# A transformer block on one core: the list scheduler's order taken from its finer model of the engines

## The chip, the cores and the metric

The kernel runs on 1 core of one Trainium2 chip. The metric is the device time of one execution in microseconds (us), the median over runs. The core has five engines with an instruction queue each: TensorE (PE, matrix products; its weight loads stand as PEld in the profile), VectorE (DVE), ScalarE (ACT), GpSimd (POOL) and SyncE (SP, which here issues nearly all transfers). An engine takes its instructions in the order of its queue, and waits at the head of it for the semaphores that the instruction names.

## The reference, cut to what matters

One block over 2048 tokens of width 1024, in float32:

```python
h = rmsnorm(x, norm_mix_g)
q, k, v, u, vg = split(h @ w_in)                  # 1024 x 2560
a_out = stick_breaking_attention(q, k, v)         # 8 heads of 64, strictly causal
b_out = spatial_gating(gelu(u), gelu(vg), ...)    # 8 groups, 128 x 128 position mixing
mix = concat(rmsnorm(a_out, g_a), rmsnorm(b_out, g_b))
x = x + mix @ w_out                               # 1024 x 1024
h = rmsnorm(x, norm_mlp_g)
x = x + square(relu(h @ w_up)) @ w_down           # 1024 x 4096 x 1024
return rmsnorm(x, norm_final_g)
```

In the attention, the weight of key s for query t is sigmoid(z_ts) times the product of (1 - sigmoid(z_tj)) over the keys j between s and t: a running product along the keys, from the last to the first.

## The kernel before, in words

**The arithmetic.** Every large product is made from operands that are split in two parts, high and low (`split`, lines 78 to 85: ACT writes the high part at line 81 or 84, DVE subtracts it and writes the low part at line 82 or 85), and three passes on PE: high by high, high by low, low by high (`mm3`, lines 89 to 91). One pass multiplies a 128 x 128 tile into 512 columns.

**Stages.** Tokens go in four chunks of 512. `proj` (line 109) makes the projections, first of chunks 0 and 1 together, then of chunk 2 and of chunk 3; the split weights `w_in` are kept in DRAM (`wi_d`) after their first use and loaded from there later, and q, k and v go out to DRAM. `attention` (line 316) is a generator of small steps. A step works on 128 queries against 512 keys of one head: `weigh` loads the keys `kt` (line 329, 2 buffers), the values `vt` (line 331, 3 buffers) and the queries `qt`, makes the scores `z` on PE (lines 345, 346, and 348 on the diagonal), two sigmoids on ACT (`kk` at 351, `b` at 353), the running product `pr` on DVE (a scan, lines 356 and 359) and the weights `b` by a product on DVE (357 and 360). Five steps later `turn` transposes them on PE (line 370) and splits them into `aT`, and two steps after that `gather` multiplies them with `vt` into `av` (lines 388 and 389). `Out` (line 462) takes a chunk's attention and gating results back from DRAM, splits and transposes them (`operands`; 32 matmuls of one column against a column of ones, line 498, sum the squares of the attention output for its norm, whose mean is taken by the DVE instruction `ra_m` at line 73), multiplies them with `w_out` (`product`) and normalizes and transposes the result (`turn`, line 567). The MLP runs plainly for chunks 0 and 1 (`up_plain`, `down_plain`) and, for chunks 2 and 3, by a scheme with seven products in the place of eight (`up_seven`, `down_seven`, with operands from `Rights` and `Lefts`).

**Order in the program.** `together` (line 916) walks through two generators, a main one and the attention as a side one, and takes a given number of side steps (1.0, 0.5 or 0.49) for each main one. So the program text interleaves projection with attention of earlier chunks, then `Out` with attention, then the plain MLP with attention.

**Order on the engines.** The text isn't yet the order of the queues. When the `with tile.TileContext(...)` block of `kernel` closes, the library's list scheduler walks through the program on a model of the engines: whenever an engine of the model is free, it takes the first instruction in the order of the text whose operands the model holds to be finished and whose buffers it holds to be free. The order in which the model took them is the order of the engine's queue on the chip, for all five queues, SP's transfers included; semaphores are placed afterwards, so that the result is right whatever the order. Instructions that the model held to be ready early so stand early, and if on the chip their operands come later, what is behind them waits. The library has two such models: a coarse one, which is the default, and a finer one that it otherwise uses to simulate the timeline of a finished program.

## Time and profile before

| | us |
|---|---|
| median of 3 runs | 2582.65 |
| the three runs | 2588.75, 2582.65, 2582.36 |
| the profiled execution's own time | 2588.74 |
| its span, from the first to the last instruction | 2587.0 |
| PE busy in the span | 2461.0 |
| DVE busy | 1709.0 |
| ACT busy | 1152.8 |
| moved by DMA | 446.58 MB |
| mean granted share of PE's full clock | 0.974 |

Busy time is the time in which an engine had an instruction in execution; matmuls overlap each other, so the time of one matmul is longer than the distance between two. A row of a timeline gives start, duration, engine, line and operation, and in brackets the idle time of the engine before it with the instruction that ended it.

### The profile page before, as it was taken

The page shows a single profiled execution, that of the slowest core. Times are in us where ns is not written, and L with a number is a line of the kernel's source. Part 1 is how long each engine was busy: PE and PEld are TensorE (multiplying, and loading weights), DVE is VectorE, ACT ScalarE, POOL GpSimd, SP SyncE. Part 2 cuts the span into 40 slices and gives each one's busy share as a digit, 9 for nine tenths or more (in the row PEclk, how much of TensorE's full clock was granted, in tenths as well). Part 3 has the DMA queues.
Part 4 walks back from the last instruction along what each step waited for, and adds up shares of the span by engine and source line. Part 5 has one row for each costly group of instructions (what it writes and reads, how often), then busy time and mean ns, then how long its engine had stood idle before and what let it go on. Part 6 is the DMA issues. An engine that isn't in the chain of part 4 may idle for free.

```text
span 2587.0 us, 30340 instructions
## 1 busy us (share of the span) xinstructions
PE 2461.0 (95%) x11424; PEld 2001.7 (77%) x11424; DVE 1709.0 (66%) x2280; ACT 1152.8 (45%) x2004; POOL 307.6 (12%) x255
## 2 busy tenths in 40 slices
PE   8899999998989999999999899999988999999997
PEld 7687677776867888888878688888877888778886
DVE  3743448867668666666666788745557666577787
ACT  4432335546345555555563554422235445433333
POOL 1100001100010000000000000000013232223331
PEclk9999999999989999999999999999999999999999
DMA  9736787678664343433363733255323444573422
GB/s 373 245 130 208 226 258 247 196 215 280 220 216 150 115 127 115 126 119 118 122 208 136 255 115 118 85 211 207 136 82 130 153 152 151 216 260 127 163 98 98
DMA packets 158225, 446.58 MB, mean 173 GB/s; under 512 B 12544, under 2 KB 28928, under 8 KB 138624
## 3 DMA queue, kind: packets, MB, share of 16 engines
q1 hardware_dynamic: 149744, 417.39, 48.4%
q0 software_dynamic: 4032, 25.17, 2.4%
q10 hardware_dynamic: 4304, 2.10, 0.3%
q8 instruction: 90, 1.47, 0.2%
q14 instruction: 55, 0.45, 0.1%
HBM read 314.59 MB, written 130.02 MB: 172 GB/s over the span
## 4 chain that ended last, share of the span: by engine, by line
PE 77%; DVE 13%; DMA 3%; issue 2%; ACT 2%; POOL 2%; SPq 0%; POOLq 0%; DVEq 0%; ACTq 0%
PE mm L91 21%; PE mm L90 21%; PE mm L89 21%; PE tr L370 4%; PE av L388 2%; PE av L389 2%; PE z L346 2%; PE z L345 2%; DVE pr L359 2%; DVE w L82 2%; DVE pr L356 1%; DVE aT L82 1%; DVE t L82 1%; DMA w_in<-wi_d 1%; PE mm L498 1%
## 5 line engine op out<-in xcount | busy, mean ns | idle before, releaser
L91 PE MATMUL mm<-t,t 128*128 128x512 f32 x1280 | 504.4, 394 | 0.0
L90 PE MATMUL mm<-t,t 128*128 128x512 f32 x1280 | 503.9, 394 | 0.2
L89 PE MATMUL mm<-t,t 128*128 128x512 f32 x1280 | 503.0, 395 | 0.2 <-DVE t L663 0.2
L351 ACT ACTIVATE kk<-z 128x512 f32<-128x512 f32 (+2 forms) x320 | 171.4, 536 | 359.3 <-PE z L346 242.6
L359 DVE TENSOR_TENSOR_SCAN pr<-kk,pr,zeros 128x513 f32<-128x513 f32 x192 | 247.0, 1287 | 121.2 <-ACT kk L351 120.8
L91 PEld LDWEIGHTS mm<-t,t 128*128 128x128 f32 x1280 | 242.7, 190 | 52.5
L90 PEld LDWEIGHTS mm<-t,t 128*128 128x128 f32 x1280 | 242.8, 190 | 52.3 <-DVE t L85 1.0
L89 PEld LDWEIGHTS mm<-t,t 128*128 128x128 f32 x1280 | 242.8, 190 | 52.1 <-DVE t L663 0.6
L81 ACT ACTIVATE aT<-tr 128x512 fp32r<-128x512 f32 (+1 forms) x320 | 172.6, 541 | 124.1 <-PE tr L370 123.8
L370 PE MATMUL tr<-ident,b 128*128 128x128 f32 x1088 | 184.4, 282 | 34.0 <-DVE aT L82 21.6
L82 DVE TENSOR_TENSOR aT<-tr,aT 128x512 fp32r<-128x512 f32 (+1 forms) x320 | 191.3, 599 | 35.9 <-ACT aT L81 35.7
L370 PEld LDWEIGHTS tr<-ident,b 128*128 128x128 f32 x1088 | 133.3, 143 | 79.0 <-DVE aT L82 28.1
L90 PE MATMUL mm<-w,w 128*128 128x512 f32 x448 | 176.5, 394 | 10.7 <-DVE w L82 9.1
L91 PE MATMUL mm<-w,w 128*128 128x512 f32 x448 | 175.4, 392 | 0.0
L89 PE MATMUL mm<-w,w 128*128 128x512 f32 x448 | 172.6, 391 | 2.3 <-ACT w L81 2.3
L353 ACT ACTIVATE b<-z 128x512 f32<-128x512 f32 (+2 forms) x320 | 170.8, 534 | 0.0
L81 ACT ACTIVATE t<-t 128x1024 fp32r<-128x1024 f32 x104 | 105.5, 1063 | 134.4 <-DMA t<-in_w_down 68.0
L356 DVE TENSOR_TENSOR_SCAN pr<-kk,zeros 128x128 f32<-128x128 f32 (+3 forms) x128 | 104.5, 819 | 88.1 <-ACT kk L351 87.5
L82 DVE TENSOR_TENSOR w<-raw,w 128x512 fp32r<-128x512 f32 (+1 forms) x135 | 152.4, 1130 | 3.3 <-ACT w L81 2.8
L81 ACT ACTIVATE w<-raw 128x512 fp32r<-128x512 f32 (+1 forms) x135 | 106.4, 800 | 105.3 <-PE mm L91 85.8
L91 PE MATMUL mm<-t,w 128*128 128x512 f32 x380 | 149.7, 394 | 3.5 <-DVE w L82 3.5
L89 PE MATMUL mm<-t,w 128*128 128x512 f32 x380 | 150.7, 397 | 0.1
(214 smaller groups left out, 4776.8 us busy)
## 6 DMA issues: line engine op xcount, KB each, us to landing
w_in<-wi_d SPq DMA_DIRECT2D x40, 1024.0 KB, 7.8
kt<-k_d SPq DMA_DIRECT2D x160, 256.0 KB, 5.0
t<-in_w_down SPq DMA_DIRECT2D x28, 1024.0 KB, 5.2
s_d<-acts SPq DMA_DIRECT2D x16, 1792.0 KB, 6.2
raw<-s_d SPq DMA_DIRECT2D x28, 1024.0 KB, 4.8
t<-wo_d SPq DMA_DIRECT2D x24, 1024.0 KB, 7.1
wi_d<-w_in POOLq DMA_DIRECT2D x20, 1024.0 KB, 8.3
vt<-v_d SPq DMA_DIRECT2D x80, 256.0 KB, 2.7
```

What stands on the lines that cost most here:

```text
L81: nc.scalar.activation(hi, src, AF.Copy)
L82: nc.vector.tensor_tensor(lo, src, hi.bitcast(F32), ALU.subtract)
L89: nc.tensor.matmul(ps, lh, rh, start=first, stop=False, skip_group_check=more)
L90: nc.tensor.matmul(ps, lh, rl, start=False, stop=False, skip_group_check=more)
L91: nc.tensor.matmul(ps, ll, rh, start=False, stop=last, skip_group_check=more)
L345: nc.tensor.matmul(z[:, :Z], ql, kt[:, 0, :Z], start=True, stop=False)
L346: nc.tensor.matmul(z[:, :Z], ql, kt[:, 1, :Z], start=False, stop=not diag)
L351: nc.scalar.activation(kk[:, :L], z[:, :L], AF.Sigmoid, scale=-QK_SCALE)
L353: nc.scalar.activation(b[:, :L], z[:, :L], AF.Sigmoid, scale=QK_SCALE)
L356: nc.vector.tensor_tensor_scan(pr[:, L - 1::-1], kk[:, L - 1::-1], zeros[:, :L], 1.0, ALU.mult, ALU.add)
L359: nc.vector.tensor_tensor_scan(pr[:, ::-1], kk[:, ::-1], zeros, carry[tb], ALU.mult, ALU.add)
L370: nc.tensor.transpose(tr[:, tb * P:(tb + 1) * P], bs[tb][:, j * P:(j + 1) * P], ident)
```

## The change

The scheduler's model is exchanged: one argument where the context is opened. No line of the block itself changes.

```diff
-    with tile.TileContext(nc) as tc:
+    with tile.TileContext(nc, schedule_with_timeline_sim=True) as tc:
         block_kernel(tc, *args)
```

## Rows read from the trace of the kernel before

**Rows 1.** The page's first part: busy time, share of the span, instructions.

```profile
PE 2461.0 (95%) x11424; PEld 2001.7 (77%) x11424; DVE 1709.0 (66%) x2280; ACT 1152.8 (45%) x2004; POOL 307.6 (12%) x255
```

**Rows 2.** Stretches: length; PE, PEld, DVE, ACT, POOL busy (count); PEclk, DMA share, GB/s.

```profile
0.00:250.00 250.00, 231.19 (x1025) 189.53 (x1026) 117.86 (x188) 93.55 (x136) 25.74 (x51) 0.98 0.67 238
250.00:600.00 350.00, 324.62 (x1578) 256.16 (x1576) 224.25 (x384) 153.82 (x329) 23.64 (x29) 0.98 0.76 233
600.00:850.00 250.00, 221.41 (x1057) 178.26 (x1057) 189.20 (x277) 128.61 (x258) 20.14 (x24) 0.90 0.63 205
850.00:1350.00 500.00, 496.62 (x2461) 408.27 (x2459) 323.88 (x414) 286.91 (x547) 11.45 (x13) 1.00 0.41 128
1350.00:1480.00 130.00, 117.89 (x548) 94.53 (x547) 88.96 (x119) 55.21 (x101) 5.20 (x7) 0.91 0.63 212
1480.00:1920.00 440.00, 439.22 (x2055) 362.85 (x2054) 287.44 (x368) 148.34 (x238) 18.30 (x23) 0.99 0.40 138
1920.00:1960.00 40.00, 25.76 (x93) 19.03 (x92) 31.12 (x35) 21.28 (x30) 14.30 (x11) 0.86 0.28 106
1960.00:2250.00 290.00, 290.00 (x1260) 237.33 (x1259) 180.72 (x239) 142.63 (x240) 78.52 (x57) 1.00 0.44 159
2250.00:2587.00 337.00, 314.27 (x1360) 255.72 (x1359) 265.59 (x261) 122.45 (x131) 110.32 (x40) 0.98 0.41 154
```

**Rows 3.** Timeline of PE, 355 to 358 us.

```profile
355.60 0.47 PE L89 MATMUL mm<-w_in,hT 128*128 128x512 f32 x1
...
357.44 0.33 PE L370 MATMUL tr<-ident,b 128*128 128x128 f32 x1 [0.90 <-DVE b L357]
357.53 0.48 PE L89 MATMUL mm<-w_in,hT 128*128 128x512 f32 x1
357.85 0.39 PE L90 MATMUL mm<-w_in,hT 128*128 128x512 f32 x1
```

**Rows 4.** PE's waits: us in total, times, longest us.

```profile
PE tr L370 <- DVE aT L82: 21.6, 23, 1.8
PE tr L370 <- DVE b L357: 9.8, 16, 1.5
...
PE z L345 <- DMA kt<-k_d: 7.4, 2, 3.8
```

**Rows 5.** Timeline of DVE, 752 to 754 us.

```profile
752.12 0.16 DVE L73 TENSOR_SCALAR ra_m<-mm 128x4 f32<-128x4 f32 x1 [6.72 <-PE mm L498]
752.20 0.28 DVE L357 TENSOR_TENSOR b<-b,pr 128x127 f32<-128x127 f32 x1
752.40 1.55 DVE L356 TENSOR_TENSOR_SCAN pr<-kk,zeros 128x256 f32<-128x256 f32 x2
```

**Rows 6.** Timeline of PE, 745 to 753 us.

```profile
745.27 6.82 PE L498 MATMUL mm<-ones,t 128*128 128x1 f32 x32
...
752.52 0.63 PE L90 MATMUL mm<-t,t 128*128 128x512 f32 x1
```

**Rows 7.** Line 498, who waited for it: us in total, times.

```profile
  DVE ra_m L73: 24.1, 4
```

**Rows 8.** The chain that ended last, line 498, three of four: start, us.

```profile
645.49 6.62 PE mm L498 x32
...
1353.83 6.62 PE mm L498 x32
...
1704.17 4.12 PE mm L498 x32
```

**Rows 9.** Timeline of all engines around 1935 us.

```profile
1934.18 2.36 DVE L82 TENSOR_TENSOR t<-w,t 128x1024 fp32r<-128x1024 f32 x2 [3.38 <-DMA out_y<-t]
```

**Rows 10.** Waits of SP's queue: us in total, times, longest us.

```profile
SPq L331 <- PE av L389: 411.2, 58, 24.5
```

**Rows 11.** Timeline of all engines, 617 to 631 us.

```profile
617.64 7.17 SPq L329 DMA_DIRECT2D kt<-k_d  x2
...
630.89 0.55 PE L345 MATMUL z<-kt,qt 128*128 128x256 f32 x1 [3.79 <-DMA kt<-k_d]
```

## The prediction

> **What bounds the kernel now.** Read first the page's table of engines [rows 1]: TensorE (PE) is busy 2461.0 of 2587.0 us. All that better cover could give back is therefore the remaining 126.0 us and what the clock cost. Then read the stretches [rows 2], cut where the stages change. They fall into two kinds. From 850 to 1350, 1480 to 1920 and 1960 to 2250 us PE is busy 496.62 of 500, 439.22 of 440 and 290.00 of 290 us: 4.16 us idle in 1230. No order of its instructions can shorten these unless it shortens the work, and the work is the same. The idle time lies in the others: 18.81 us in 0 to 250, 25.38 in 250 to 600, 28.59 in 600 to 850, 12.11 in 1350 to 1480, 14.24 in 1920 to 1960 and 22.73 in 2250 to 2587. In the third and fourth the granted clock is 0.90 and 0.91 as well: part of the time PE ran at the lower of its two levels, 1.2 instead of 2.4 GHz.
>
> Then ask of each idle piece: was other work ready on the same engine, placed behind the instruction that waited? Only those pieces can change when the order does. The timeline of PE shows the pattern [rows 3]: a transpose of the attention (line 370) waits 0.90 us for VectorE's (DVE's) product `b`, and directly behind it stand passes of a projection whose operands had been in use since 355.60. The scheduler puts nothing on an engine that its model says isn't ready while something else is. So its model had the transpose's operand done sooner than the chip did.
>
> **The change, part by part.** It adds and removes no instruction, no byte and no buffer; every engine keeps its work. It changes the time at which the scheduler believes each result is there, and so the order on five queues, SP's DMAs included. Its cost is the sum of the waits that it moves.
>
> (a) *Transposes placed too early.* PE waited 21.6 us (23 times) at line 370 for the split half `aT` and 9.8 us (16 times) for `b` [rows 4], 31.4 us together. Not all have something ready behind them. Around 730 to 745 the operands of the next matmuls are themselves late (DVE is busy 189.20 of 250 us there, a larger share than in any other stretch but the two short of full at the end [rows 2]), so moving a transpose back would only move the wait. In 250 to 600, where the projection's weights are mostly resident, the wait goes. The ends are 0 (all waits are real dependences) and 31.4 us; I take a third, 10 us, since the stretch 250 to 600 holds about a quarter to a third of the idle time outside the start-up and the tail.
>
> (b) *DVE held by one small instruction.* In the operand stage of each `Out`, 32 matmuls of one column (line 498) sum the squares of the attention output. They take 6.82 us [rows 6], and DVE's 0.16 us instruction `ra_m` stands at the head of its queue for 6.72 of them [rows 5], though a product `b` and two scans stand right behind and need nothing from those matmuls: they run at once when it is through, 0.28 and 1.55 us, 1.8 together. This happens 4 times, 24.1 us in all [rows 7]. A model that prices 32 such matmuls at what they take would put the scans first. By the chain of waits [rows 8] the first of the four lies at 645 us, the third at 1354 and the last at 1704; the second is that of [rows 6]. The first three lie in stretches where DVE limits PE, the fourth where PE is full. In each of the three between 1.8 us (the rows shown) and the whole wait, some 6, would be done earlier. Ends: 0 and 3 x 6 = 18 us. I take 6, a third, near the rows shown (3 x 1.8 = 5.4): PE works in that time anyway, and only what it waits less afterwards counts.
>
> (c) *The clock.* In 600 to 850 and 1350 to 1480 the granted shares of 0.90 and 0.91 mean that 20% of 250 and 18% of 130 us, 73 us, were at the lower level; if PE worked throughout, half of that, 37 us, is what it cost. The level shows in one pass of 512 columns, which takes 0.63 us in [rows 6] and 0.39 in [rows 3]. Fewer waits could win some of it back; a worse order could lose as much. Ends: 37 us won, 37 lost. I take 0, because the work around the falls stays: the clock is low after the 6.82 us of line 498 [rows 6], in which PE was busy, with one column at a time.
>
> By the Trainium skill's TensorE: Matmul & The Clock Gate, section HAM oscillation, idle gaps between bursts bring the lower clock back and its price is half of the time spent there; by that rule, a third of the waits gone would give a third of (c) too, 12 us more, and the sum below would be 28 instead of 16. The trace agrees on the two levels (0.63 and 0.39 us a pass); against the idle gaps as the only cause stand the 6.82 busy us of line 498, after which the clock is low.
>
> (d) *The start-up, the change of stage at 1930 and the tail.* Here I cost the change at nothing. At 1934 DVE waits 3.38 us for an output's DMA to free a buffer [rows 9], in the stretch with 14.24 us of idle PE: a dependence, not an order. Ends: these 3.38 us won, if the buffer is given out in another order, and as much lost.
>
> (e) *SP's queue.* SP is the one queue where an instruction that waits holds many others: it stood 411.2 us at line 331 until a `vt` buffer was free [rows 10]. Today this reaches PE in two waits for `kt`, 7.4 us [rows 4]. A new order of DMAs can change this in either direction: ends 7.4 won and, below, 22 lost; I take 0.
>
> Sum: 10 + 6 = 16 us, 0.6%. The profiled execution's own time is 2588.74 us (span 2587.0 and 1.7 around it); the median of the three runs shown is 2582.65, 6.1 lower. So 2588.7 - 16 = 2572.7 for an execution like the profiled one and 2566.6, rounded 2567, for the median.
>
> **The rivals.** 0.3%, 7.7 us, is about what a measurement of this kernel can tell from no change.
>
> *No change within that.* The order may differ in many places, yet the waits are dependences and buffers: the transposes wait for DVE whatever the order, `ra_m` hides behind line 498 in which PE works anyway. For: nearly half of the kernel, the 1230 us with 4.16 idle, can't move, and DVE at 189.20 of 250 us has little room where it matters. Against: [rows 3] and [rows 5], where ready work stood behind. Also here: the two models may agree on every order that counts, so that the change does nothing. Time: 2582.65 less 0 to 7, say 2580. The Trainium skill's Perfetto Trace Analysis, section Optimization Strategy, reads a gap that repeats on the engine that should be full as a sign of too few buffers for the next tile; the trace agrees in part: SP's 58 waits for a `vt` buffer [rows 10] are such gaps, and an order leaves the number of buffers alone. I give this case 0.25.
>
> *Slower: loads of `kt` behind a waiting `vt`.* The place is SP's queue between 250 and 850 us, where projections and attention share it. The mechanism shows once, in [rows 11]: the issue of two halves of `kt` takes from 617.64 until 624.81, because SP was held in between, and PE idles 3.79 us until 630.89, when the second has landed. If the finer model issues the `vt` loads (3 buffers) a little earlier relative to `kt` (2 buffers), this wait repeats; each costs 3.7 us (7.4 by 2). It decides from the third added wait if nothing is won in (a) and (b) (11.1 us, over the 7.7), from the seventh if the 16 us are. With six and nothing won: 2582.65 + 22 = 2605. For it: SP waits at line 331 in 58 cases already, so little is needed. Against it: a model closer to the chip should rather see the held queue. I give slower by over 0.3% 0.28.
>
> *Much faster.* All of (a) and (b) and a third of (c): 31.4 + 18 + 12 = 61 us, 2522. This needs every wait to have ready work behind it, and [rows 9] and the DVE share in [rows 2] speak against. It is within the chance of faster, at 0.05.
>
> **How the numbers follow.** Faster by over 0.3% has 0.47: 0.42 for the forecast and 0.05 for the much faster case; no change 0.25; slower 0.28. The forecast's own range is 2545 (the upper ends of (a) and half of (b) and (c) lie beyond it) to 2575. The range over all cases goes from 2543 to 2606: it takes in the slower rival at six waits and leaves out the much faster case and a slower one with more than six.
>
> **What would show it.** Right: in the changed profile PE's waits at line 370 fall from 31.4 towards 20 us; DVE's wait at `ra_m` before line 498's end falls from 24.1 towards 5 with scans or products run in those 6.8 us; the stretches 850 to 1350 and the like keep their lengths, and the gain sits in the stages that are 250 to 850 and 1350 to 1480 now. Wrong: if PE's waits for `kt` or `w_in` grow past 20 us, the slower rival holds; if the waits fall and the span doesn't, they were only moved; if the full stretches change their length, the order reached work that I took as fixed.

## The result, and the profile after

The changed kernel takes 2517.15 us (median of 4 runs, 2511.05 to 2518.97) against 2583.74 (4 runs, 2582.36 to 2588.75; the three shown ahead of the prediction had 2582.65) for the kernel before: a ratio of 0.9731, with a 95% interval of 0.9716 to 0.9745. It is 66.6 us faster; the forecast was 16, and 2517 lies below the range. The profiled execution took 2518.97 us. The first part of its page, against [rows 1]:

```profile
PE 2430.1 (97%) x11424; PEld 1991.5 (79%) x11424; DVE 1694.0 (67%) x2280; ACT 1145.2 (45%) x2004; POOL 309.8 (12%) x255
```

The same instructions; PE is busy 30.9 us less, and idle 87.1 us of 2517.2 in place of 126.0. The mean granted clock is 0.982 (before 0.974).

To see where the time came from, both traces are cut at the ends of the same matmuls, so that each stretch holds the same work on PE. First the kernel before (columns as in [rows 2]): the gates (the columns for u and vg in the first projections) of chunks 0 and 1, the projections of chunks 2 and 3 with the attention beside them, everything behind them.

```profile
52.70:163.70 111.00, 99.33 (x450) 81.49 (x450) 62.14 (x107) 44.25 (x65) 12.76 (x17) 0.95 0.58 204
253.90:611.70 357.80, 332.46 (x1616) 262.98 (x1617) 234.93 (x397) 160.37 (x341) 24.11 (x30) 0.98 0.75 230
611.70:2577.30 1965.60, 1893.43 (x8770) 1546.42 (x8768) 1351.32 (x1691) 895.97 (x1523) 256.65 (x172) 0.97 0.45 154
```

Then the same three in the changed kernel:

```profile
53.90:148.60 94.70, 94.70 (x451) 79.25 (x450) 61.73 (x108) 44.04 (x64) 13.37 (x20) 1.00 0.61 231
238.80:559.30 320.50, 316.28 (x1616) 260.20 (x1617) 234.86 (x398) 158.08 (x339) 28.36 (x30) 0.99 0.79 257
559.30:2506.70 1947.40, 1882.42 (x8769) 1540.52 (x8768) 1336.26 (x1687) 890.44 (x1522) 252.40 (x171) 0.98 0.45 155
```

The gates of the start-up fall by 16.3 us (15.1 of it are left at the end of the first projections, 253.9 to 238.8), the projections of chunks 2 and 3 by 37.3, and the other 1966 us by 18.2. That is 70.6 us and not 66.6, because it compares the two profiled executions, and that of the kernel before took 5 us more than its median. In the second stretch PE's idle time falls from 25.3 us (357.80 less 332.46) to 4.2.

PE's waits in the changed kernel, against [rows 4]:

```profile
PE tr L370 <- DVE aT L82: 17.8, 18, 2.2
...
PE z L345 <- DMA kt<-k_d: 2.7, 2, 1.6
...
PE tr L370 <- DVE b L357: 1.8, 2, 0.9
```

The transposes' waits for `aT` and `b` fall from 31.4 to 19.6 us. The 436.3 us that SP's queue stands at `vt`, against [rows 10], are more than before:

```profile
SPq L331 <- PE av L389: 436.3, 69, 21.3
```

Who waited for line 498, against [rows 7]:

```profile
  DVE ra_m L73: 8.0, 3
```

That wait falls from 24.1 to 8.0 us. Yet the stretches in which the first three of [rows 7] lay shrink little: the output products of chunks 0 and 1 by 1.8 us (218.9 to 217.1), that of chunk 2 by 3.1 (98.0 to 94.9). First the one of chunks 0 and 1 before, then in the changed kernel:

```profile
611.70:830.60 218.90, 190.31 (x917) 152.75 (x916) 163.14 (x246) 111.91 (x226) 18.75 (x22) 0.90 0.66 216
```

```profile
559.30:776.40 217.10, 186.66 (x909) 149.63 (x909) 160.44 (x243) 111.47 (x226) 16.07 (x22) 0.90 0.65 218
```

### The profile page after: what moved, and what is told of

Read it like the earlier page. It is cut to its first block, busy times and chain, and to the rows that moved or that the text cites. A ratio compares the mean times of both kernels' runs of the same rounds, so it can differ in the third digit from the quotient of the medians.

```text
span 2517.2 us, 30341 instructions
## 1 busy us (share of the span) xinstructions
PE 2430.1 (97%) x11424; PEld 1991.5 (79%) x11424; DVE 1694.0 (67%) x2280; ACT 1145.2 (45%) x2004; POOL 309.8 (12%) x255
## 4 chain that ended last, share of the span: by engine, by line
PE 86%; DVE 8%; issue 3%; DMA 3%; ACT 1%; POOL 0%; POOLq 0%; SPq 0%; DVEq 0%; ACTq 0%
PE mm L91 24%; PE mm L90 24%; PE mm L89 23%; PE tr L370 4%; PE av L389 2%; PE z L346 2%; PE av L388 2%; PE z L345 2%; DVE w L82 2%; DVE t L82 1%; DVE pr L359 1%; PE mm L498 1%; DVE aT L82 1%; PE mm L263 1%; DMA t<-b_d 1%
## 5 line engine op out<-in xcount | busy, mean ns | idle before, releaser
L82 DVE TENSOR_TENSOR aT<-tr,aT 128x512 fp32r<-128x512 f32 (+1 forms) x320 | 191.1, 598 | 21.6 <-ACT aT L81 21.3
L370 PE MATMUL tr<-ident,b 128*128 128x128 f32 x1088 | 180.9, 279 | 21.9 <-DVE aT L82 17.8
L90 PE MATMUL mm<-w,w 128*128 128x512 f32 x448 | 176.4, 394 | 8.8 <-DVE w L82 8.6
L91 PE MATMUL mm<-w,w 128*128 128x512 f32 x448 | 175.6, 392 | 0.0
L82 DVE TENSOR_TENSOR t<-t,t 128x1024 fp32r<-128x1024 f32 x104 | 123.6, 1225 | 39.1 <-ACT t L81 19.4
```

Source lines behind the costliest of these rows:

```text
L82: nc.vector.tensor_tensor(lo, src, hi.bitcast(F32), ALU.subtract)
L90: nc.tensor.matmul(ps, lh, rl, start=False, stop=False, skip_group_check=more)
L91: nc.tensor.matmul(ps, ll, rh, start=False, stop=last, skip_group_check=more)
L370: nc.tensor.transpose(tr[:, tb * P:(tb + 1) * P], bs[tb][:, j * P:(j + 1) * P], ident)
```

## The experiments

**How an order is moved from one kernel to the other.** Both kernels trace the same instructions in the same order; only the queues differ. So the order that the finer model gave one queue can be written into the kernel before as a chain: each instruction of the queue must be issued behind the one ahead of it, with no wait for its end. The scheduler's model then lists the other queues around that, so their orders can change as well: a run that holds one queue doesn't change that queue alone. The edit, the same in all runs named pin_ or free_ (the text of an order is left out):

```diff
+ORDERS = {
+    "SP": "...",
+}
+
+def forced_order(tc):
+    traced = tc.nc.cur_bb.bb.instructions
+    for text in ORDERS.values():
...
+        for first, then in zip(order, order[1:]):
+            tc.add_manual_dep(then, first.name, mybir.DependencyInfo(
+                mybir.DependencyClass.NoSync, mybir.DependencyReason.DATA), reason="order")
...
         together(down_seven(loads, rm))
+    forced_order(tc)
```

All runs in one table. Start is the end of the first projections, the second column the stretch with the projections of chunks 2 and 3, the third the rest up to the last matmul, from the profiled execution and cut at the same matmuls as above (in ra_11 more attention falls into the second). Ratios are to the kernel before on the same chip.

| run | us | ratio, 95% interval | start | proj 2, 3 | rest |
|---|---|---|---|---|---|
| before (profiled) | | | 253.9 | 357.8 | 1965.6 |
| changed (profiled) | 2517.15 | 0.9731, 0.9716 to 0.9745 | 238.8 | 320.5 | 1947.4 |
| pin_sp | 2584.06 | 0.9992, 0.9983 to 1.0002 | 251.6 | 344.3 | 1983.8 |
| pin_pe | 2635.79 | 1.0192, 1.0176 to 1.0208 | 252.9 | 375.5 | 1988.2 |
| pin_act | 2616.04 | 1.0121, 1.0105 to 1.0137 | 247.1 | 359.4 | 1994.8 |
| pin_dve | 2625.05 | 1.0153, 1.0138 to 1.0168 | 254.8 | 354.8 | 2001.7 |
| pin_all | 2522.02 | 0.9751, 0.9734 to 0.9767 | 238.7 | 322.6 | 1949.9 |
| free_pe | 2565.43 | 0.9926, 0.9911 to 0.9941 | 243.4 | 328.3 | 1979.3 |
| free_sp | 2607.49 | 1.0088, 1.0073 to 1.0103 | 243.8 | 389.7 | 1963.9 |
| free_dve | 2545.67 | 0.9846, 0.9831 to 0.9860 | 241.2 | 326.2 | 1961.4 |
| pair_act_sp | 2566.42 | 0.9920, 0.9905 to 0.9935 | 244.4 | 330.8 | 1974.4 |
| pin_first | 2570.24 | 0.9937, 0.9923 to 0.9952 | 238.4 | 359.3 | 1964.5 |
| pin_proj | 2551.08 | 0.9867, 0.9851 to 0.9884 | 253.6 | 323.5 | 1958.3 |
| pin_late | 2566.14 | 0.9916, 0.9902 to 0.9931 | 253.2 | 355.5 | 1947.3 |
| stores_pool | 2576.04 | 0.9961, 0.9946 to 0.9976 | 253.6 | 343.0 | 1963.7 |
| win_pool | 2599.50 | 1.0044, 1.0027 to 1.0061 | 255.1 | 363.9 | 1968.1 |
| split_pool | 2591.42 | 1.0022, 1.0012 to 1.0032 | 259.2 | 356.5 | 1964.6 |
| undo_sp | 2554.98 | 0.9877, 0.9858 to 0.9897 | 239.1 | 358.4 | 1949.9 |
| stores_fine | 2518.55 | 0.9744, 0.9730 to 0.9759 | 238.9 | 321.3 | 1944.1 |
| ra_11 | 2520.40 | 0.9738, 0.9723 to 0.9752 | 238.8 | 329.8 | 1934.5 |

**One queue at a time.** The theories were: SP (loads behind waiting stores), PE (transposes placed too early, as the prediction had it), ACT, and joint.

```diff
+    "SP": "...",      # pin_sp; "PE", "ACT" or "DVE" in its place for the other three
```

> The kernel before (coarse model), with SyncE's queue alone held to the order that the finer model gave it; the coarse model lists the other four engines around that. Theory SP (loads stood behind waiting stores on SyncE's queue, so attention's k and v blocks came late and in bursts): the stretch of proj of chunks 2 and 3 falls from 356 us to about 320, the start-up of the gates stays at 111, in all 2535 to 2550 us. Theory PE (the transposes stood too early in TensorE's own queue): that stretch stays within 5 us of 356, in all 2575 to 2585. Theory ACT (ScalarE's order alone): no change here. Theory joint (no one engine's order carries it): under 10 us, 2573 to 2585.

> The kernel before, with TensorE's queue alone held to the finer model's order. Theory PE: the waits of the transposes on aT and b (31.4 us) go, and the stretch of proj of chunks 2 and 3 falls from 356 us to about 320; the gates' start-up stays; in all 2535 to 2550 us. Theory SP: the loads are as late as before, so TensorE waits elsewhere (for k blocks and scores) and the stretch stays above 345; in all 2570 to 2590. Theory ACT: no change. Theory joint: under 10 us either way, or some us slower.

> The kernel before, with ScalarE's queue alone held to the finer model's order. Theory ACT (in the gates of chunks 0 and 1 a weight's split stood ready behind a sigmoid that waited for VectorE): that stretch falls from 111 us to about 96; in the stretch of proj of chunks 2 and 3 nothing, in all about 2568 us. If ScalarE's order carries the later stretch too: 2530 to 2545. Theory SP or PE for the start-up: the stretch stays at 108 to 111, in all 2578 to 2585.

> The kernel before, with VectorE's queue alone held to the finer model's order. If the gates' start-up hangs on VectorE's order (evacuations before or after the multiplications that the sigmoids wait for): that stretch falls from 111 us to about 96, in all about 2568. If the scans of the attention steps were bunched by VectorE's own order: the stretch of proj of chunks 2 and 3 falls by 20 us or more, in all 2550 or below. By theories SP, PE and ACT: within 5 us of 2583.

No queue brings the gain alone, and three of the four make the kernel slower; these three totals lie outside every range that was written down for them. SP's order wins 13.5 us in the projections of chunks 2 and 3 and loses 18.2 behind them; ScalarE's wins 6.8 us in the start-up, half of what is to be had there. PE's order is the telling one. Its waits in the stretch of 375.5 us:

```profile
PE z L364 <- DMA qt<-q_d: 31.7, 2, 18.2
PE mm L108 <- DMA w_in<-wi_d: 11.9, 7, 3.3
...
PE tr L389 <- DVE aT L101: 1.2, 1, 1.2
```

(Lines stand 19 higher in this kernel.) The transposes no longer wait, as theory PE said, but the time is not won: PE now stands at scores whose queries `qt` haven't been loaded. With PE's order the waits only moved. Theory PE falls, and of the others only joint is left for the whole of the gain.

**All queues, and all but one.**

```diff
+    "PE": "...", "DVE": "...", "ACT": "...", "SP": "...", "POOL": "...",    # pin_all
+    "DVE": "...", "ACT": "...", "SP": "...",                                # free_pe
+    "PE": "...", "DVE": "...", "ACT": "...",                                # free_sp
+    "PE": "...", "ACT": "...", "SP": "...",                                 # free_dve
```

> The control: the coarse model, with all five queues held to the finer model's orders. If the orders alone carry the gain (every theory so far): 2515 to 2520 us, 2.7% below before, every stretch as in the changed kernel. If something else that the finer model sets (buffers, semaphores) carries part of it: above 2525.

> VectorE's, ScalarE's and SyncE's queues held to the finer model's orders; TensorE's queue is listed by the coarse model around them. Theory PE-last (what the coarse model gets wrong is where TensorE's queue puts its attention steps among the projection's passes; it shows only when the others keep step): TensorE's waits on aT and b stay, the stretch of proj of chunks 2 and 3 stays above 350 us, in all 2575 to 2640. Theory chain (the order of the work around TensorE is what counts; TensorE's own place follows): 2515 to 2530.

> TensorE's, VectorE's and ScalarE's queues held to the finer model's orders; SyncE's (and GpSimd's) are listed by the coarse model around them. If SyncE's order is needed (loads behind waiting stores): the waits on kt, qt, vt and w_in come back, the stretch of proj of chunks 2 and 3 is 330 to 350 us, in all 2530 to 2570. If SyncE's order matters only as a follower of the others (pin_sp alone brought nothing): 2515 to 2525.

> TensorE's, ScalarE's and SyncE's queues held to the finer model's orders; VectorE's is listed by the coarse model around them. If VectorE's order follows from the others: 2515 to 2530. If the scans, products and evacuations have to stand in the finer model's order: VectorE holds scores or evacuations back, TensorE waits on tr, b and aT by tens of us, in all above 2560.

GpSimd's queue, nearly idle, is left to the coarse model in the three free_ runs. With all five held, the coarse model gives the changed kernel's time within the intervals: the orders alone carry the gain. Each of the three queues left to the coarse model costs something, SP's by far the most (ScalarE's was not tried): 85 us (2607.5 against 2522.0), 67 of them in the stretch of the projections. PE's waits there, in free_sp (lines 21 higher):

```profile
PE av L409 <- ACT aT L102: 21.4, 1, 21.4
PE mm L110 <- DMA w_in<-wi_d: 21.2, 8, 5.6
PE z L366 <- DMA qt<-q_d: 15.1, 1, 15.1
```

With SP's order in, and PE's or DVE's left to the coarse model, the stretch still comes to 328.3 and 326.2 us, some 30 of its 37 us; without SP's it is longer than before. By the traces PE, VectorE and ScalarE take their instructions in the same order in free_sp as in pin_all and in the changed kernel, so these 67 us come from SP's queue (and GpSimd's) alone. But the order that SP gets there is a third one: in chunk 2 it stands 29.7 us at `vt` and 23.9 at the stores. None of the three free_ totals came out in a range that was given for it.

**Place by place.** All five queues held, but each order is cut to what one part of the program issues: the first projections (pin_first), the projections of chunks 2 and 3 with their attention (pin_proj), all behind them (pin_late). The edit is that of pin_all with shorter orders:

```diff
+    "PE": "...", "DVE": "...", "ACT": "...", "SP": "...", "POOL": "...",
```

> The coarse model, with all five queues held to the finer model's orders only for what the first pass over the projections (chunks 0 and 1) issues. Theory stages (the gain is a sum of places that don't depend on each other): the gates of chunks 0 and 1 fall from 111 to about 95 us and nothing later changes, in all 2566 to 2570 us. Theory whole (a new order in one place is given back in the next): above 2575.

> The coarse model, with all five queues held to the finer model's orders only for what the projections of chunks 2 and 3 and the attention beside them issue. Theory stages: that stretch falls from 358 to about 320 us, the start-up stays at 254, the rest stays, in all 2543 to 2550 us. Theory whole: the gain is given back in the stretch of the attention's output products, in all above 2565.

> The coarse model, with all five queues held to the finer model's orders only for what is issued behind the projections (output products, both MLPs, the attention beside them). Theory stages: the start-up and the projections stay at 254 and 358 us; the rest gives 14 to 18 us (the 66.6 less the 15.5 and 34.7 of the two stretches held alone), in all 2567 to 2572. Theory whole (the later gain follows from an earlier order): within 5 us of 2585.

Each part wins about what it won in the changed kernel, and little elsewhere (at most 7.3 us, in the rest of pin_proj): 15.5, 34.7 and 21.3 us (medians, each against the kernel before on the same chip), 71.5 in sum against 66.6 for the whole. So the places add up, while the queues don't. The medians of pin_first and pin_proj are just above what was expected and pin_late's just below; pin_late's rest, 1947.3 us, is the changed kernel's 1947.4.

**What happens on SP's queue in the projections.** SP's queue in the kernel before, in chunk 2 (the rows end some us ahead of [rows 3]):

```profile
326.55 3.60 SPq L121 DMA_DIRECT2D w_in<-wi_d  x4
330.20 1.32 SPq L329 DMA_DIRECT2D kt<-k_d  x2
331.56 0.59 SPq L331 DMA_DIRECT2D vt<-v_d  x1
332.20 0.45 SPq L334 DMA_DIRECT2D qt<-q_d  x1
334.16 0.58 SPq L329 DMA_DIRECT2D kt<-k_d  x1
349.46 1.73 SPq L226 DMA_DIRECT2D v_d<-qkv_st  x2
351.24 0.68 SPq L329 DMA_DIRECT2D kt<-k_d  x1
```

The issues come in blocks. Four weight tiles of 1 MB go out at once, and behind them the blocks of k, v and q for one unit of the attention. Then SP stands from 334.7 to 349.46 at a store of v whose data aren't there. Behind it waits the other half of the `kt` of the next unit. The issues from 326 to 335 us, with the median time from issue to landing:

```profile
w_in<-wi_d SPq DMA_DIRECT2D x4, 1024.0 KB, 10.8
kt<-k_d SPq DMA_DIRECT2D x3, 256.0 KB, 15.7
```

ScalarE and VectorE meanwhile:

```profile
347.95 0.69 ACT L84 ACTIVATE qkv_st<-mm,x_r 128x512 fp32r<-128x512 f32 x1 [11.74 <-PE mm L91]
```

```profile
348.68 0.75 DVE L85 SCALAR_TENSOR_TENSOR qkv_st<-mm,x_r,qkv_st 128x512 fp32r<-128x512 f32 x1 [11.75 <-ACT qkv_st L84]
```

Both run dry for 11.7 us while PE works through passes of the projection alone. The unit whose loads were issued from 330.20 to 332.20 has its four scores on PE within 2 us, from 351.16 on; ScalarE and VectorE have four steps at once, and PE waits at the transposes: the 0.90 us of [rows 3] is one of these. The next unit, whose half of `kt` was held behind the store, has its scores from 360.94 on. PE shows no wait for `kt`: in the order of its queue there was nothing but passes there. In the changed kernel, at the same stores of v, a unit's loads are issued between two stores, with no weight tile just ahead:

```profile
317.53 0.59 SPq L329 DMA_DIRECT2D kt<-k_d  x1
318.21 0.55 SPq L226 DMA_DIRECT2D v_d<-qkv_st  x1
318.81 0.59 SPq L329 DMA_DIRECT2D kt<-k_d  x1
```

```profile
kt<-k_d SPq DMA_DIRECT2D x2, 256.0 KB, 5.5
```

These two places are far apart in how long the loads took to land, but they are not typical: behind three weight tiles at 271 us `kt` takes 14.9 us to land in the changed kernel too, and over the whole of chunk 2 the median is 10.7 us before and 11.3 there. What differs over the whole of chunk 2 is how long SP stands at the stores of q, k and v until VectorE has made their data. Before, then in the changed kernel:

```profile
SPq L185 <- DVE qkv_st L82: 28.1, 4, 14.3
SPq L226 <- DVE qkv_st L85: 22.8, 4, 12.8
```

```profile
SPq L226 <- DVE qkv_st L85: 4.9, 2, 4.4
SPq L185 <- DVE qkv_st L82: 2.9, 1, 2.9
```

So 50.9 us become 7.8. The bursts go with it: the longest time on PE from the scores of one step to those of the next is 24.9 us before (326.3 to 351.2) and 11.4 in the changed kernel.

Two runs test this, one with a change of queue instead of order and one with two queues' orders:

```diff
+        stores = nc.gpsimd if cs[0] > 0 else nc.sync
...
-                        nc.sync.dma_start(dst[2 * e + j, :, :, c * TC:(c + 1) * TC].rearrange("x d t -> d x t"),
+                        stores.dma_start(dst[2 * e + j, :, :, c * TC:(c + 1) * TC].rearrange("x d t -> d x t"),
...
-            queue = nc.scalar if cs[-1] == NC - 1 else nc.sync
+            queue = nc.scalar if cs[-1] == NC - 1 else stores
...
-                nc.sync.dma_start(b_d[t:t + P], u)
+                stores.dma_start(b_d[t:t + P], u)
```

> The kernel before under the coarse model, with the stores of q, k, v and b in the projections of chunks 2 and 3 issued on GpSimd's queue, so that no load on SyncE's queue stands behind a store that waits for VectorE. Theory SP (stores ahead of loads): TensorE's waits there (25 us) fall by half or more, the stretch falls from 358 to 325 to 345 us, in all 2550 to 2572. If what holds SyncE's queue is the loads that wait for their own buffers (vt for the product on TensorE, w_in for the passes): the stretch stays above 350, in all 2575 to 2590.

```diff
+    "ACT": "...", "SP": "...",
```

> The coarse model, with ScalarE's and SyncE's queues alone held to the finer model's orders. Theory pair (loads in time are of use only if ScalarE takes the scores as they come; SyncE alone gave 13.6 us in the stretch of proj of chunks 2 and 3, and with ScalarE and VectorE 29.6): 25 to 30 us in that stretch, 7 to 10 in the start-up, in all 2545 to 2575. If VectorE's order is needed as well: within 5 us of the 344 us of SyncE alone there, in all 2575 to 2600.

With the stores on GpSimd's queue, under the coarse model, the stretch falls by 14.8 us, all of it in chunk 2 (181.1 to 165.2); the stores of v in chunk 3 were on ScalarE's queue before, and stay there. By the medians the kernel gains 9.7 us: the stretch, 343.0, is within what theory SP said, the total of 2576 lies above its range and in the rival's. PE's waits from the projection of chunk 2 to the end of that of chunk 3:

```profile
PE mm L89 <- DMA w_in<-wi_d: 9.4, 8, 1.9
...
PE tr L371 <- DVE aT L82: 0.7, 1, 0.7
PE tr L371 <- DVE b L358: 0.5, 2, 0.3
```

In the kernel before the same stretch has 9.3 us for `b` and 4.1 for `aT`. The coarse model lists all queues anew here, but no order is imposed. So the transposes stop waiting when the stores leave SP's queue: the releaser that the rows name, DVE, was not the cause but a late link of the chain. SP's order alone (pin_sp) could not do this: SP still stands at these stores for 35.1 us in chunk 2, which takes 178.9. With ScalarE's order as well (pair_act_sp) it stands there for 7.3, and chunk 2 takes 164.8; the pair came out as expected.

Is it the DMA engines' time that is lost while SP stands? Chunk 2's part in the kernel before, the changed one and undo_sp (below), in that order, each cut at the same matmuls; the last column but one is the mean busy share of the DMA engines:

```profile
253.90:435.00 181.10, 165.38 (x786) 128.37 (x787) 107.26 (x191) 77.32 (x170) 11.29 (x17) 0.96 0.78 241
```

```profile
238.80:396.30 157.50, 153.28 (x786) 125.69 (x787) 106.57 (x190) 75.28 (x168) 12.55 (x17) 0.99 0.86 282
```

```profile
239.10:421.70 182.60, 164.51 (x789) 131.51 (x789) 102.21 (x187) 70.86 (x161) 12.40 (x17) 0.94 0.74 231
```

Length by share: the DMA engines are busy for 141, 135 and 135 us, and idle for 40, 22 and 47. The transfers' own time hardly differs. That doesn't say that they set the length, as PE is busy 97% of the stretch once the order is right. The thought that with 135 us of transfers in 157 of work a hole of 15 us in the issues can hardly be made up for is an argument that no run tests.

Chunk 3 stayed at 178 us with the stores moved. A run on its weight loads:

```diff
-                nc.sync.dma_start(w.bitcast(F32), wi_d[col, k2])
+                nc.gpsimd.dma_start(w.bitcast(F32), wi_d[col, k2])
```

> The kernel before under the coarse model, with the weight loads of the projections of chunks 2 and 3 issued on GpSimd's queue, so that they stand behind nothing on SyncE's. Theory loads (in chunk 3 TensorE's 5.3 us of waits for w_in, and the attention steps that bunch up behind them, are the cause): proj of chunk 3 falls from 177 to 165 to 170 us, chunk 2 by 0 to 10, in all 2560 to 2575. Theory order of the k, q and v blocks (SyncE's order helps by these): chunk 3 stays above 174, in all 2578 to 2588.

A miss: 2599.5 us. PE's waits for `w_in` grow from 5.3 to 12.8 us in the two projections, and 8.8 us for an operand `hT` come on top. On GpSimd's queue, too, the loads stand behind heads that wait: it stands for 73.4 us at a copy of zeros into `aT` (line 375) and for 47.4 at `ln_r`, so the run doesn't test loads that stand behind nothing. In chunk 3 SP's order by itself does help (pin_sp, 165.4 us in place of 176.7), but which of its issues is open.

The reverse test, in the changed kernel:

```diff
     with tile.TileContext(nc, schedule_with_timeline_sim=True) as tc:
...
+    "SP": "...",
```

The order is the one of the kernel before, cut to what the projections of chunks 2 and 3 and their attention issue.

> The changed kernel (finer model), with SyncE's queue alone held to the coarse model's order, and only for what the projections of chunks 2 and 3 and the attention beside them issue; the finer model lists the other engines around that. Theory SP: the loads stand behind waiting stores again, SyncE sits for 10 us and more at single stores, and the stretch grows from 320 us to 345 to 360, in all 2540 to 2560. Theory rest (with the other queues in the finer order the stores are ready when SyncE comes to them): the stretch stays below 328, in all 2515 to 2525.

The stretch goes back to 358.4 us, as theory SP said, the start-up and the rest stay within 3 us, and the kernel loses 37.8 us of its 66.6 (2554.98 against 2517.15). SP stands at the stores of q, k and v for 41.1 us in chunk 2, and the longest distance between two steps' scores is 27.3 us. By the traces the orders of PE, ScalarE and VectorE in the stretch are then others than the changed kernel's too; so the run shows that with SP's old order the gain of this stretch is gone, even with the other queues listed by the finer model, and not what SP's order costs by itself. SP's queue in it (lines 19 higher):

```profile
320.17 0.58 SPq L348 DMA_DIRECT2D kt<-k_d  x1
337.35 1.73 SPq L245 DMA_DIRECT2D v_d<-qkv_st  x2
339.13 0.68 SPq L348 DMA_DIRECT2D kt<-k_d  x1
```

The same hole, now 16.6 us, at the same store of v, with the half of `kt` behind it.

**The start-up.** ScalarE's queue in the kernel before, in the gates of chunks 0 and 1:

```profile
102.32 0.63 ACT L232 ACTIVATE gelu_t<-vnx 128x512 f32<-128x512 f32 x1
106.05 0.63 ACT L234 ACTIVATE gelu_t<-gelu_t 128x512 f32<-128x512 f32 x1 [3.10 <-DVE gelu_t L233]
...
107.82 1.04 ACT L81 ACTIVATE w_in<-stx 128x1024 fp32r<-128x1024 f32 x1
```

And in the changed kernel:

```profile
95.83 1.99 ACT L81 ACTIVATE w_in<-stx 128x1024 fp32r<-128x1024 f32 x2
98.92 0.63 ACT L234 ACTIVATE gelu_t<-gelu_t 128x512 f32<-128x512 f32 x1 [1.11 <-DVE gelu_t L233]
```

Before, the sigmoid (line 234) stands at the head for 3.10 us and the next weight's copy, with no wait of its own, comes after it; in the changed kernel two copies are made in the same hole. The Trainium skill's Perfetto Trace Analysis, section Tensor Engine Instruction, calls VectorE's, ScalarE's and GpSimd's queues strictly first in, first out; the row at 106.05 agrees. To test it without an order, the copies were given to GpSimd:

```diff
-            split(w[:, 0], w[:, 1], st)
+            if late:
+                nc.gpsimd.tensor_copy(w[:, 0], st)
+                nc.vector.tensor_tensor(w[:, 1], st, w[:, 0].bitcast(F32), ALU.subtract)
+            else:
+                split(w[:, 0], w[:, 1], st)
```

> The kernel before under the coarse model, with the weights' copies of all columns after the first in the start-up made by GpSimd in place of ScalarE. Theory ACT (a weight's copy stands ready on ScalarE behind a sigmoid that waits for VectorE): TensorE's waits for w_in (6.6 us) go and the gates of chunks 0 and 1 fall from 111 to 96 to 104 us, in all 2570 to 2578. Theory buffers (the copy is late because its buffer or its load is late): the stretch stays at 108 to 111 or grows by GpSimd's slower copy, in all 2580 to 2600.

A miss as well: the start-up grows to 259.2 us. GpSimd's queue shows why:

```profile
108.87 0.92 POOL L75 TENSOR_TENSOR ln_r<-ln_m,mhalf 128x1 f32<-128x1 f32 x1 [4.05 <-DVE ln_m L73]
109.75 2.48 POOL L126 CAST w_in<-stx 128x1024 fp32r<-128x1024 f32 x2
```

The copies now stand behind an `ln_r` that waits 4.05 us for VectorE: one waiting head was exchanged for another. The total, 2591.4, lies in the range of theory buffers, though not for the reason given there. So this run says nothing on how much of the start-up hangs on the copies. What is shown is that the five orders together give its 15 us (pin_first, 238.4), ScalarE's alone 6.8 (pin_act, 247.1), and all but one of PE's, DVE's and SP's 10.1 to 12.7 (free_sp to free_dve); how the half beyond ScalarE's divides is open.

**Beyond the change.** Two versions of the changed kernel:

```diff
-    R_A, R_O, R_U = 1.0, 0.5, 0.49
+    R_A, R_O, R_U = 1.1, 0.5, 0.49
```

> The changed kernel (finer model) with 1.1 attention steps in place of 1.0 per step of the projections: some 8 steps of 12 instructions move out of the stretch of the output products' operands, where TensorE idles 23 us. If that idle time is attention that has no other work beside it: 2505 to 2514 us, the stretch falls by 8 to 15 us and the projections grow by 4 to 6. If VectorE (79% busy beside the projection of chunk 3) can't take more there: 2515 to 2530.

The same edit as in stores_pool, under the finer model:

> The changed kernel (finer model), with the stores of q, k, v and b in the projections of chunks 2 and 3 on GpSimd's queue. If the finer model's order has already taken the cost of stores ahead of loads: 2513 to 2522 us, the stretch within 3 us of 320. If a part is left (TensorE idles 4 us there): 2505 to 2513.

Neither is faster than the changed kernel (0.9738 and 0.9744 against 0.9731, intervals overlapping). With more attention beside the projections, where VectorE is busy, these grow by 9.3 us and what lies behind them shrinks by 12.9; the stretch of the operands of chunks 0 and 1 gives 7 of them (131.1 to 124.1), just under the 8 to 15 that were hoped for. Moving the stores gains nothing once the order is right: its stretch is 321.3 us, the changed kernel's 320.5.

## Why the prediction was wrong

The side was right, the size was not: 16 us were forecast and 66.6 measured. Of the 70.6 us between the two profiled executions, 37.3 lie in the projections of chunks 2 and 3, 15.1 in the start-up and 18.2 behind both.

**Step (e), SP's queue, is the one that failed.** The prediction priced it at 0, with 7.4 us as the most to be won, because only two waits for `kt` reached PE by name. That took the releaser named in a wait at PE for its cause. It also looked at the wrong wait of SP: the 411.2 us at `vt` of [rows 10], on which the slower rival and the case of no change leaned too, are 436.3 us in the faster kernel, and they are waits of SP, not gaps on PE. What the runs showed in its place: SP stood at stores whose data were late (50.9 us in chunk 2, 7.8 in the changed kernel), loads were issued late and in blocks, the attention ran dry and then came in bursts, and the bursts appeared at PE as waits at transposes, for DVE. The stretch in which this happens gave 37.3 us. Moving the stores alone, with no order imposed, wins 14.8 of them (stores_pool); with SP's old order put back and the other queues listed around it, 37.9 are lost (undo_sp). How much between the two is SP's alone, and what in SP's order helps chunk 3, is open. The hint was in rows that were read: the stretch 250 to 600 has the highest DMA share of all, 0.76 [rows 2].

**Step (a), the transposes.** The number held (31.4 to 19.6 us; a fall towards 20 was forecast) and the reason didn't: that is luck. In the projections, where the waits went, it was not the transpose's place in PE's queue: with PE's order from the finer model (pin_pe) those waits went and the same stretch grew by 17.7 us. Of the 17.8 us for `aT` that are left, 9.3 lie in the output products of chunks 0 and 1, where the prediction had said that they would only move.

**Step (b), `ra_m`.** The order changed as forecast (24.1 to 8.0 us; a part of it because line 498 took 3.7 us in place of 6.8 at 701 us, where the clock was high), and the stretches of the first three waits gave 4.9 us between them for all causes together; 6 were counted for this one alone. No run took it by itself.

**Step (c), the clock, was taken at 0.** In the two stretches that (c) priced, 0 held: cut at the same matmuls, the granted clock is 0.90 and 0.93 in them, before and after. The reason given for it misread [rows 6]. The clock was low before line 498 began, behind transposes that had waited 1.29 and 1.82 us, and the 6.82 us are those of 32 such matmuls at the lower level (3.73 and 3.62 at the higher, in the changed kernel). So these rows don't speak against idle gaps. The fourth of the four does: the granted clock was 1.00 when line 498 began at 1704.01 and 0.50 behind it, with no idle time on PE ahead. The last pass ahead of line 498 at 745, then the fourth with a pass on either side:

```profile
744.84 0.63 PE L388 MATMUL av<-aT,vt 128*128 128x512 f32 x1
```

```profile
1703.79 0.39 PE L90 MATMUL mm<-t,t 128*128 128x512 f32 x1
1704.01 4.28 PE L498 MATMUL mm<-ones,t 128*128 128x1 f32 x32
1708.73 0.63 PE L90 MATMUL mm<-t,t 128*128 128x512 f32 x1
```

By the mean granted clock of the whole kernel the time at the lower level would have cost 67.3 us before (0.026 of 2587.0) and 45.3 after (0.018 of 2517.2) had PE worked throughout: up to 22.0 us came back, nearly all of it outside those two stretches. Of it 5.6 lie in the gates of the start-up alone (0.95 to 1.00 of 111 us), where PE's 11.7 idle us went to 0. The Trainium skill's rule that the prediction cited, idle gaps bring the lower clock back (TensorE: Matmul & The Clock Gate, HAM oscillation), asked for a third of (c) if a third of the waits went; PE's idle time fell by 31% (126.0 to 87.1) and the lost clock by 33%, and in the stretch of line 498 neither moved (28.6 and 30.4 us idle). For the whole kernel the rule was nearer than the 0 taken.

**Step (d), places costed at nothing.** The wait for the output's DMA stayed, 3.38 and now 3.35 us, as a dependence should. But the start-up, priced at nothing with 3.38 us as the most for all of (d), gave 15.1. (d) rested on [rows 9], which lie at the change of stage; the gates of chunks 0 and 1 had 11.7 us of idle PE, and ScalarE's queue there shows the copy behind the sigmoid. The change of stage gave 5.3 us (38.2 to 32.9) and the last stage 5.8 (323.7 to 317.9); these were not taken apart.

**What was right.** The stretches in which PE was full kept their length: the first half of the plain MLP 508.5 and 508.0 us, `up_seven` behind its first round 290.3 and 290.9. The gain sits where PE was idle.

**The rivals.** The slower one, `kt` behind a waiting queue, didn't come (PE waits 2.7 us for `kt` in the changed kernel), but its place was the right one: in free_sp and pin_pe, 21.7 and 48.8 us slower than before, PE stands long for late loads, of `qt` and `w_in`. The much faster case had the time, 2522, and a chance of 0.05, from a sum of (a), (b) and (c) that is not where the time came from: luck as well.

## What to carry to other kernels

A wait at the full engine names the last link, not the cause: follow it back until a queue stands still, then look at what is queued behind its head, above all loads behind a store whose data are late, and read the DMA share of that stretch. An order is one thing over all queues: to find which queue matters, put one queue's old order back into the good set as well as its new order into the old set, since one queue's good order alone was worth nothing or cost up to 1.9% here. Hold the other queues while you do it: a scheduler that lists them anew changes more than the queue under test. Places along the program, by contrast, could be tested apart, and nearly added up.

## What the runs showed of the hardware that was not expected

- The same 1616 matmuls kept PE busy 332.46 us before and 316.28 after, and 332.06 with SP's order put back. The granted clock, 0.96 and 0.99 in the parts of chunks 2 and 3 before and 0.99 and 1.00 after, accounts for some 7 of these 16 us; where the rest lies was not followed up.
- The Trainium skill's DMA: Bandwidth & Descriptors, section Issuing engines are not separate DMA queues, says that transfers from several engines share the same DMA engines and that spreading the issues saves only the issue time. No row here tests the first: the blocks of 256 KB that landed after 15.7 us behind four weight tiles, and after 5.5 without, were all issued by SP. On the second the runs show one thing more to be saved: moving stores to GpSimd's queue took 14.8 us off a stretch, as loads no longer stood behind a waiting head.
- GpSimd's copy of 128 x 1024 took 1205 ns (mean of 9) and ScalarE's 1.04 us: over nine copies 1.5 us, against the 5.3 us by which the start-up grew in split_pool.
